# Slice 0 in halves over the hardware queues, slice 1 over the software queue: how a weight-gradient matmul starts

## The chip, the cores and the metric

One core of a Trainium2 chip. The metric is device time in microseconds (us) per execution. The kernel before takes 175.97 us (median of 6 runs, 175.87 to 176.45). In profiles, times count from the start of the profiled span, which is about 1.8 us shorter than the execution.

## The reference, cut to what matters

```python
batch, m, k, n = 16, 512, 1024, 768          # input [16,512,1024], grad_output [16,512,768], float32
grad_weight = np.einsum('bmk,bmn->kn', input, grad_output)     # [1024, 768]
```

Call the input X and the gradient G, both flattened to 8192 rows. The result is the transpose of X times G, a sum over 64 slices of 128 rows. One slice needs 12 matmuls of 512 columns: 8 "wide" ones (X's eight blocks of 128 columns against G's first 512 columns; A is blocks 0 to 3, B is 4 to 7) and 4 "narrow" ones (N: G's last 256 columns in two interleaved sets against X's two halves).

## The kernel before: the parts that matter

All inputs are float32 in HBM and are multiplied in bf16. The transfers that this kernel issues from GpSimd (the software queue, called the stream below) deliver bf16. Those that it issues from SyncE and ScalarE (the hardware queues) deliver float32, which VectorE (DVE) and ScalarE (ACT) round. Slice 0 comes that way, and X of slice 1. In the profile lines PE is TensorE, PEld its weight loads, POOL is GpSimd; a transfer "lands" when its last part has arrived.

```python
ORDER = ("A1! B1 N1 B2! N2 A2 N3! A3 B3 A4! B5 N5 B6! N7 A6 N8! A9! B10 N9 B12! N12! A12! "
         "B15 AB17! n17! AB26! n26! AB41! n41! AB47 A50! B50! N64!").split()
WARMUP = [512] * 10 + [128] * 2
# ... cut ...
xf = [head.tile([P, K], f32, name=f"xf{s}") for s in range(2)]
gf = head.tile([P, N], f32, name="gf")
nc.sync.dma_start(out=gf[:, 0:NA], in_=G[0:P, 0:NA])          # wide G of slice 0
nc.scalar.dma_start(out=xf[0], in_=X[0:P, :])                 # X of slice 0, whole rows of 4 KB
nc.sync.dma_start(out=gf[:, NA:N], in_=G[0:P, NA:N])          # narrow G of slice 0
nc.scalar.dma_start(out=xf[1], in_=X[P : 2 * P, :])           # X of slice 1
# ... warm-up matmuls on ones ...
for s in range(1, S):                                         # the software stream
    gt = xg.tile([P, N], bf16, name="gt")
    nc.gpsimd.dma_start(out=gt, in_=G[s * P : (s + 1) * P, :])
    if s > 1:
        xs[s] = xg.tile([P, K], bf16, name="xt")
        nc.gpsimd.dma_start(out=xs[s], in_=X[s * P : (s + 1) * P, :])
```

`ORDER` is the schedule of the matmuls. "B10" takes B up to slice 10, "!" closes the part: its four PSUM banks are evicted (copied or added into SBUF by DVE and ACT) and set free. The kernel uses eight banks, so two parts can be open at a time.

## Time and profile before

| what | before |
|---|---|
| span, TensorE busy | 174.3 us, 97% |
| first useful matmul | 5.32 us |
| last matmul starts | 171.25 us |
| stream | one slice (G and X) per 2.2 us |
| TensorE | one slice per 2.59 us (12 x 0.216) |

The profile's chain, timeline and landings are read in the prediction below.

### The profile page before, as it was taken

The page shows a single profiled execution, that of the slowest core. Times are in us where ns is not written, and L with a number is a line of the kernel's source. Part 1 is how long each engine was busy: PE and PEld are TensorE (multiplying, and loading weights), DVE is VectorE, ACT ScalarE, POOL GpSimd, SP SyncE. Part 2 cuts the span into 40 slices and gives each one's busy share as a digit, 9 for nine tenths or more (in the row PEclk, how much of TensorE's full clock was granted, in tenths as well). Part 3 has the DMA queues.
Part 4 walks back from the last instruction along what each step waited for, and adds up shares of the span by engine and source line. Part 5 has one row for each costly group of instructions (what it writes and reads, how often), then busy time and mean ns, then how long its engine had stood idle before and what let it go on. Part 6 is the DMA issues. An engine that isn't in the chain of part 4 may idle for free.

```text
span 174.3 us, 2013 instructions
## 1 busy us (share of the span) xinstructions
PE 169.9 (97%) x793; PEld 78.4 (45%) x808; DVE 61.3 (35%) x103; ACT 6.2 (4%) x12; POOL 66.7 (38%) x129
## 2 busy tenths in 40 slices
PE   8999999999999999999999999999999999999993
PEld 3444444444444444444444444444444444444463
DVE  0655582883940039300000662200560003931122
ACT  2640000000000000000000000000000000000000
POOL 7444434444444444444444444444274200000000
PEclk9999999999999999999999999999999999999999
DMA  5999999999999999999999999999999990085623
GB/s 192 276 208 209 207 209 208 208 208 209 207 208 209 207 208 210 207 209 209 206 209 208 208 210 207 207 209 208 207 209 209 207 202 11 0 190 160 170 86 120
DMA packets 25048, 33.35 MB, mean 191 GB/s; under 512 B 6480, under 2 KB 16592, under 8 KB 25040
## 3 DMA queue, kind: packets, MB, share of 16 engines
q0 software_dynamic: 18000, 28.65, 89.9%
q10 hardware_dynamic: 4448, 2.10, 4.7%
q1 hardware_dynamic: 2592, 2.49, 4.2%
q8 instruction: 6, 0.10, 0.2%
q14 instruction: 2, 0.02, 0.0%
HBM read 58.72 MB, written 3.15 MB: 355 GB/s over the span
## 4 chain that ended last, share of the span: by engine, by line
PE 97%; issue 0%; DVE 0%
PE bank L127 63%; PE bank L134 32%; PE bank L81 3%; DVE acc L118 0%
## 5 line engine op out<-in xcount | busy, mean ns | idle before, releaser
L127 PE MATMUL bank<-gt,xt 128*128 128x512 bf16 (+2 forms) x515 | 108.3, 367 | 0.5
L127 PEld LDWEIGHTS <-xt 128*128 128x128 bf16 x524 | 50.2, 98 | 57.2
L118 DVE TENSOR_TENSOR acc<-bank,acc 128x512 f32<-128x512 f32 (+2 forms) x62 | 37.9, 667 | 73.4 <-PE bank L127 72.9
L134 PE MATMUL bank<-xt,gt 128*128 128x512 bf16 x242 | 54.8, 379 | 0.3
L97 POOL DMA_DIRECT2D xt<-in_input_dram x62 | 33.1, 533 | 38.7 <-DMA xt<-in_input_dram 36.5
L92 POOL DMA_DIRECT2D gt<-in_grad_output_dram x63 | 33.8, 536 | 31.2 <-DMA gt<-in_grad_output_dram 24.9
L134 PEld LDWEIGHTS <-gt 128*128 128x128 bf16 x252 | 24.6, 98 | 29.7
L118 DVE TENSOR_TENSOR acct<-bank,acct 128x512 f32<-128x512 f32 x24 | 15.7, 682 | 30.0 <-PE bank L134 29.9
L81 PE MATMUL bank<-const-bfloat16-1.0 128*128 128x512 bf16 (+1 forms) x12 | 4.6, 574 | 0.8 <-PEq L263 0.8
L81 PEld LDWEIGHTS <-const-bfloat16-1.0 128*128 128x128 bf16 x12 | 1.6, 140 | 3.5 <-issue 3.5
L122 DVE COPY acc<-bank 128x512 f32<-128x512 f32 x4 | 2.7, 687 | 1.0 <-PE bank L127 1.0
L180 DVE STREAM_TRANSPOSE turned<-acct 128x512 f32<-128x512 f32 x4 | 2.9, 715 | 0.1
L127 PEld LDWEIGHTS <-x 128*128 128x128 bf16 x16 | 1.6, 98 | 1.9 <-DVE x L107 0.2
L107 DVE CAST g<-gf 128x256 bf16<-128x256 f32 x2 | 0.6, 290 | 4.7 <-DMA gf<-in_grad_output_dram 4.7
L124 ACT COPY acc<-bank 128x512 f32<-128x512 f32 x4 | 2.1, 589 | 1.3 <-PE bank L127 1.3
L127 PE MATMUL bank<-gt,x 128*128 128x512 bf16 x8 | 2.1, 379 | 0.0
L127 PE MATMUL bank<-g,x 128*128 128x512 bf16 x8 | 2.0, 398 | 0.0
L122 DVE COPY acct<-bank 128x512 f32<-128x512 f32 x2 | 1.3, 686 | 1.3 <-PE bank L134 1.3
L107 ACT CAST x<-xf 128x256 bf16<-128x256 f32 x4 | 1.4, 409 | 0.0
L107 ACT ACT_TABLE_LOAD x1 | 1.3, 1283 | 1.7 <-PEq L263 1.7
L124 ACT COPY acct<-bank 128x512 f32<-128x512 f32 x2 | 1.1, 588 | 1.5 <-PE bank L134 1.5
L107 DVE CAST x<-xf 128x256 bf16<-128x256 f32 (+1 forms) x5 | 1.0, 260 | 0.0
(8 smaller groups left out, 3.3 us busy)
## 6 DMA issues: line engine op xcount, KB each, us to landing
xt<-in_input_dram POOLq DMA_DIRECT2D x62, 256.0 KB, 8.5
gt<-in_grad_output_dram POOLq DMA_DIRECT2D x63, 192.0 KB, 8.5
out_dram<-acc SPq DMA_DIRECT2D x13, 128.0 KB, 2.7
xf<-in_input_dram ACTq DMA_DIRECT2D x2, 512.0 KB, 5.1
out_dram<-turned ACTq DMA_DIRECT2D x4, 256.0 KB, 3.4
gf<-in_grad_output_dram SPq DMA_DIRECT2D x1, 256.0 KB, 3.9
out_dram<-acc SPq DMA_DIRECT2D x1, 256.0 KB, 2.0
gf<-in_grad_output_dram SPq DMA_DIRECT2D x1, 128.0 KB, 4.7
```

The source lines that it names most:

```text
L81: nc.tensor.matmul(wps[:, 0:cols], ones, nc.const_aps.tensor(1.0, (P, cols), bf16), start=True, stop=True,)
L92: nc.gpsimd.dma_start(out=gt, in_=G[s * P : (s + 1) * P, :])
L97: nc.gpsimd.dma_start(out=xs[s], in_=X[s * P : (s + 1) * P, :])
L107: copy(out=dst[:, c0:c1], in_=src[:, c0:c1])
L118: nc.vector.tensor_add(out=dst, in0=src, in1=dst)
L122: nc.vector.tensor_copy(out=dst, in_=src)
L124: nc.scalar.copy(out=dst, in_=src)
L127: nc.tensor.matmul(bank, xs[s][:, k * P : (k + 1) * P], gwide[s][:, c0:c1], start=start, stop=stop)
L134: nc.tensor.matmul(bank, gnarrow[s].rearrange("p (r t) -> p t r", t=NT)[:, t], xs[s][:, h * NA : (h + 1) * NA], start=start, stop=stop,)
L180: nc.vector.transpose(out=turned[:, h * hb : (h + 1) * hb, :, t], in_=dst.rearrange("p (b r) -> p b r", r=SQ),)
```

## The change

The intent: TensorE starts on 256 KB of G and 256 KB of X instead of 512 KB of X, so the first useful matmul comes earlier; the warm-up is shortened to match. X of slice 1 no longer passes through the hardware queue and the two rounding engines but comes as bf16 by the software queue, its later half first, since B of slice 1 needs that one first. Narrow G is used before B.

```diff
-    "A1! B1 N1 B2! N2 A2 N3! A3 B3 A4! ...
+    "A1! N1 B2! N2 A2 N3! A3 B3 A4! ...
-WARMUP = [512] * 10 + [128] * 2
+WARMUP = [512] * 9 + [128] * 3
...
-    nc.scalar.dma_start(out=xf[0], in_=X[0:P, :])
+    nc.scalar.dma_start(out=xf[:, 0:NA], in_=X[0:P, 0:NA])
     nc.sync.dma_start(out=gf[:, NA:N], in_=G[0:P, NA:N])
-    nc.scalar.dma_start(out=xf[1], in_=X[P : 2 * P, :])
+    nc.scalar.dma_start(out=xf[:, NA:K], in_=X[0:P, NA:K])
...
-        if s > 1:
-            xs[s] = xg.tile([P, K], bf16, name="xt")
-            nc.gpsimd.dma_start(out=xs[s], in_=X[s * P : (s + 1) * P, :])
+        xs[s] = xg.tile([P, K], bf16, name="xt")
+        for c0, c1 in ((NA, K), (0, NA)) if s == 1 else ((0, K),):
+            nc.gpsimd.dma_start(out=xs[s][:, c0:c1], in_=X[s * P : (s + 1) * P, c0:c1])
...   (first rounding of G: DVE 304 columns, ACT 208, instead of 256 each;
...    X's four first blocks alternate between DVE and ACT; the rounding of narrow G moves ahead of the first eviction; slice 1's roundings are gone)
-        "N": Part(narrow_mm, [(t, h) for h in range(KH) for t in range(NT)], narrow_dst),
+        "N": Part(narrow_mm, [(t, h) for h in reversed(range(KH)) for t in range(NT)], narrow_dst),
```

More of the change, by code (lines that the diff above doesn't have):

```diff
@@ L17 @@
 ORDER = (
-    "A1! B1 N1 B2! N2 A2 N3! A3 B3 A4! B5 N5 B6! N7 A6 N8! A9! B10 N9 B12! N12! A12! "
+    "A1! N1 B2! N2 A2 N3! A3 B3 A4! B5 N5 B6! N7 A6 N8! A9! B10 N9 B12! N12! A12! "
     "B15 AB17! n17! AB26! n26! AB41! n41! AB47 A50! B50! N64!"
 ).split()
-WARMUP = [512] * 10 + [128] * 2
+WARMUP = [512] * 9 + [128] * 3
 XBUFS = 42
@@ L67 @@
     ctx.enter_context(tc.manual_schedule(engines={E.PE, E.DVE, E.Activation}))
-    xf = [head.tile([P, K], f32, name=f"xf{s}") for s in range(2)]
+    xf = head.tile([P, K], f32, name="xf")
     gf = head.tile([P, N], f32, name="gf")
     nc.sync.dma_start(out=gf[:, 0:NA], in_=G[0:P, 0:NA])
-    nc.scalar.dma_start(out=xf[0], in_=X[0:P, :])
+    nc.scalar.dma_start(out=xf[:, 0:NA], in_=X[0:P, 0:NA])
     nc.sync.dma_start(out=gf[:, NA:N], in_=G[0:P, NA:N])
-    nc.scalar.dma_start(out=xf[1], in_=X[P : 2 * P, :])
+    nc.scalar.dma_start(out=xf[:, NA:K], in_=X[0:P, NA:K])
     ones = nc.const_aps.tensor(1.0, (P, P), bf16)
@@ L92 @@
         nc.gpsimd.dma_start(out=gt, in_=G[s * P : (s + 1) * P, :])
+        xs[s] = xg.tile([P, K], bf16, name="xt")
+        for c0, c1 in ((NA, K), (0, NA)) if s == 1 else ((0, K),):
+            nc.gpsimd.dma_start(out=xs[s][:, c0:c1], in_=X[s * P : (s + 1) * P, c0:c1])
         gwide[s] = gt[:, 0:NA]
         gnarrow[s] = gt[:, NA:N]
-        if s > 1:
-            xs[s] = xg.tile([P, K], bf16, name="xt")
-            nc.gpsimd.dma_start(out=xs[s], in_=X[s * P : (s + 1) * P, :])
-    for s in range(2):
-        xs[s] = head.tile([P, K], bf16, name=f"x{s}")
+    xs[0] = head.tile([P, K], bf16, name="x0")
     g0 = head.tile([P, N], bf16, name="g0")
@@ L107, in round_by @@
         copy(out=dst[:, c0:c1], in_=src[:, c0:c1])
-    round_by("DVE", g0, gf, 0, 256)
-    round_by("ACT", g0, gf, 256, NA)
-    round_by("DVE", xs[0], xf[0], 0, P)
-    round_by("ACT", xs[0], xf[0], 2 * P, 4 * P)
-    round_by("DVE", xs[0], xf[0], P, 2 * P)
-    round_by("DVE", xs[0], xf[0], 4 * P, 6 * P)
-    round_by("ACT", xs[0], xf[0], 6 * P, 8 * P)
+    round_by("DVE", g0, gf, 0, 304)
+    round_by("ACT", g0, gf, 304, NA)
+    for k in range(0, KS // 2, 2):
+        round_by("DVE", xs[0], xf, k * P, (k + 1) * P)
+        round_by("ACT", xs[0], xf, (k + 1) * P, (k + 2) * P)
+    round_by("DVE", g0, gf, NA, N)
+    round_by("DVE", xs[0], xf, NA, 6 * P)
+    round_by("ACT", xs[0], xf, 6 * P, K)
     def add_out(dst, src):
@@ L172, in add_slice @@
             copy_out(dst, bank, i)
-            if s == 0 and i == 0:
-                round_by("DVE", g0, gf, NA, N)
         else:
@@ L210, in bank_by_bank @@
                 add_slice(part, i, s, s == first, s == upto - 1)
-    for i, step in enumerate(ORDER):
-        if i == 2:
-            round_by("DVE", xs[1], xf[1], 4 * P, 6 * P)
-            round_by("ACT", xs[1], xf[1], 6 * P, 8 * P)
-            round_by("DVE", xs[1], xf[1], 0, 2 * P)
-            round_by("ACT", xs[1], xf[1], 2 * P, 4 * P)
+    for step in ORDER:
         close = step.endswith("!")
```

## The prediction

> **What bounds the kernel now.** I read the page of the slowest core first, then TensorE's instructions in order of time, then the start of the timeline over all engines, then the landings of the first transfers.
>
> ```profile
> span 174.3 us, 2013 instructions
> ...
> PE 169.9 (97%) x793; PEld 78.4 (45%) x808; DVE 61.3 (35%) x103; ACT 6.2 (4%) x12; POOL 66.7 (38%) x129
> ...
> PE 97%; issue 0%; DVE 0%
> ```
>
> The chain that ended last is TensorE for 97% of the span. Nothing but matmuls stands on it, so the time is: the moment at which the first useful matmul starts, plus the matmuls at their pace, plus what they wait for on the way, plus the tail of add and store. In order of time:
>
> ```profile
> 0.78 4.64 PE L81 MATMUL bank<-const-bfloat16-1.0 128*128 128x512 bf16 x12 [0.78 <-PEq L263]
> 5.32 2.04 PE L127 MATMUL bank<-g,x 128*128 128x512 bf16 x8
> 7.20 1.03 PE L134 MATMUL bank<-x,g 128*128 128x512 bf16 x4
> 8.06 1.03 PE L127 MATMUL bank<-gt,x 128*128 128x512 bf16 x4
> ```
>
> The twelve warm-up matmuls of ones (line 81) run from 0.78, the useful work starts at 5.32. From 7.20 on every group of four starts 0.86 us after the last one (0.216 us per matmul), and no row of TensorE after that shows an idle time before it. So there is no wait in the body to remove; 768 x 0.2158 = 165.7 us of the 174.3 are fixed, and the change can only move the start. The first eight took 1.88 us instead of 8 x 0.216 = 1.73: the trace's clock record begins full rate at 5.63, and single starts are 5.324, 5.686, 5.903, then 0.216 apart. The warm-up matmuls lie 0.427 apart, so until 5.63 the array runs at half pace. What released the first one:
>
> ```profile
> 4.71 0.41 ACT L107 CAST g<-gf 128x256 bf16<-128x256 f32 x1 [1.76 <-DMA gf<-in_grad_output_dram]
> 4.71 0.29 DVE L107 CAST g<-gf 128x256 bf16<-128x256 f32 x1 [4.71 <-DMA gf<-in_grad_output_dram]
> 5.00 0.15 PEld L81 LDWEIGHTS <-const-bfloat16-1.0 128*128 128x128 bf16 x1 [0.28 <-issue]
> 5.04 0.71 ACT L107 CAST x<-xf 128x256 bf16<-128x256 f32 x2
> 5.04 0.56 DVE L107 CAST x<-xf 128x128 bf16<-128x128 f32 x3
> ...
> 5.32 1.55 PEld L127 LDWEIGHTS <-x 128*128 128x128 bf16 x8 [0.17 <-DVE x L107]
> ```
>
> Wide G of slice 0 lands, is rounded (4.71), then X of slice 0 lands and is rounded (5.04), then the first weights load at 5.32, 0.17 us late against the end of the warm-up (last start 5.104 plus 128 columns at half pace, 0.107: 5.21). The landings in the trace are 4.684 (G wide), 5.017 (X of slice 0), 5.844 (G narrow), 7.027 (X of slice 1), and on the software queue 7.492 (G1), 8.462 (G2), 9.698 (X2), then 2.2 us per slice, while TensorE takes 12 x 0.216 = 2.59 us per slice.
>
> **What the Trainium skill says.** "DMA: Bandwidth & Descriptors", section "Queues, rings and completion order": each DMA engine takes turns between queues at packet granularity. The packet records agree: a 2048-byte packet of G (84 ns) and a 4096-byte packet of X (159 ns) alternate, one pair in 235 to 243 ns, so X with its double rows gets two thirds of the rate. The same page, "Latency and other measured facts", gives about 1 us to the first byte of a software DMA; here the first software packet starts at 5.275, 4.0 us after its issue at 1.23, so I don't use that figure. "TensorE: Matmul & The Clock Gate", "What's actually happening": the array runs at half rate until a free-running window of 3413 ns has been busy. The trace agrees (0.427 against 0.216 us, full rate from 5.63) but one profile can't show whether the moment is fixed. "ScalarE: Activation LUTs", "What ACT_TABLE_LOAD costs": 186 ns + 0.833 ns per element, successors overlapping by 93 ns; for 256 columns that is 0.40, the trace has 0.405 and a start-to-start of 0.31.
>
> **The change part by part.**
>
> Transfers. Before, the first useful matmul stands behind 256 KB of G and 512 KB of X. After, it stands behind 256 KB and 256 KB. An engine has 8 rows of each; a pair costs 84 + 84 = 168 instead of about 238 ns. The first packets are slow to start (the DMA share is 0.25 and 0.79 in the second and third microsecond), so I count 7 pairs: 7 x 0.07 = 0.49 us. Wide G then lands at about 4.2, X's first half one packet later at about 4.3 (5.017 before).
>
> Rounding. DVE 304 columns: 0.22 at 128 and 0.29 at 256 give about 0.31; ACT 208: 0.36. DVE starts its next piece some 0.08 us before the end (5.04, 5.18, 5.32), so X block 0 starts at about 4.25 + 0.23 = 4.48, and its weights load 0.28 later, as before: 4.76. ACT's share of G ends at 4.61. X blocks 1 and 3 (ACT) are ready at 4.8 and 5.0, ahead of their matmuls.
>
> Warm-up. One 512 becomes a 128: 0.32 us less, it ends at 5.21 - 0.32 = 4.89. The data being ready at 4.76, the warm-up decides, and the first useful matmul starts at 4.89, 0.43 earlier.
>
> What that is worth. The clock still rises at 5.63, I take it, so the matmuls from 4.89 run at half pace: starts 4.89, 5.32, then 380 columns until 5.63 and 132 at full rate, so the third starts at 5.69 against 5.903. Only half of the 0.43 is kept: **0.21 us**.
>
> Second halves. X's later half and narrow G of slice 0 are needed by the fifth matmul now (narrow goes ahead of B and takes the later half first), at 5.69 + 2 x 0.216 = 6.12. Eight further pairs per engine (46 for a 1 KB row by the 84 ns for 2 KB, estimated, + 84 = 130 ns) after about 3.9: landing near 5.3, roundings (DVE 0.28 and 0.29, ACT 0.41) done by 5.75. Slack 0.35.
>
> Banks. B of slice 0 reuses A's banks at the ninth matmul, 6.98. DVE is free at 5.75, its two evictions (0.69, 0.68) end at 6.43 and 7.03, for matmuls 9 and 11 (6.98, 7.41); ACT's (0.59) at 6.4 and 6.9 for 7.20 and 7.63. They hold.
>
> Software queue. X of slice 1 goes ahead of G2 now; hardware bytes fall from 1408 to 896 KB. The bytes read from HBM up to the end of X2 stay the same (2688 KB), so if the engines are never idle X2 lands near 9.7 again. If instead the software queue can't start before 5.275, it finds the engines almost free: some 240 KB of hardware packets that shared the time after 5.275 are gone, 0.55 us. Then G1 lands at 6.95, X1's later half at 7.55 (half of the 1.236 between G2 and X2), its earlier half at 8.2, G2 at 9.15, X2 at 10.4. Needed, at the new pace: G1 and X1's later half at 7.85, the earlier half at 9.14, G2 and X2 at 10.44. It holds, by 0.05 in the worst place. From slice 3 on the order is the old one, with 0.7 us or more to spare.
>
> Tail: the same stores and transposes. The sum is -0.21 us: 175.9 - 0.2 = 175.7.
>
> **Rivals.** (1) Slice 1 or 2 comes late: the software queue starts after 5.275, or halves cost more than half. For: the slack is 0.05 to 0.3 us in this reading. Against: equal bytes to X2. It would give the gain back: 175.9 to 176.1. (2) The data are no faster, because the slow start and not the bytes decides the landings: TensorE idles from 4.89 to about 5.2, gain 0.05 us, 175.85. For: the low DMA share until 3.0. (3) The clock's rise moves. If it came with the work and not at a fixed moment, the full 0.43 would count: 175.5; if the changed warm-up missed a window, 3.4 us at half pace would cost 1.7: 177.6. Against the latter: the array is as busy as before, and three runs before lie within 0.16 us.
>
> **Range and chances.** The likely outcomes lie from 175.5 to 176.0; runs of one kernel spread by 0.16, and another chip may add 0.1 to 0.2: 175.3 to 176.1. Two per cent is 3.5 us, more than everything that happens before the third useful matmul could give; only (3) at its worst comes near on the slow side.
>
> **What would show it.** Right: first useful matmul near 4.9, second 0.43 later, full clock at 5.63, the third near 5.7, no idle time before matmuls of slices 1 and 2; X of slice 0 landing near 4.3 and 5.3. Wrong: an idle time on a DMA at slice 1 or 2 (rival 1), between warm-up and work (rival 2), a clock record elsewhere than 5.63 (rival 3), or evictions that hold up the ninth matmul.

## The result, and the profile after

The changed kernel takes 176.62 us (median of 6 runs, 176.20 to 176.75), before 175.97; the ratio is 1.0026 (95% interval 1.0009 to 1.0044). A ratio is the mean time of one kernel's runs over the mean of the other's in the same rounds, so it is not quite the ratio of the medians. The forecast was 175.7 with a range of 175.3 to 176.1: the direction was wrong, and the time lies outside the range.

The page of the changed kernel, its span and its chain (share of the span by engine, then by line):

```profile
span 174.4 us, 2027 instructions
...
PE 81%; DMA 15%; POOL 2%; issue 1%; DVE 0%; POOLq 0%
PE bank L127 54%; PE bank L134 27%; DMA xt<-in_input_dram 15%; POOL gt L92 1%; POOL xt L95 1%; DVE acc L118 0%; POOLq L255 0%
```

Before, the chain was matmuls for 97%. Now it is followed back through 15% of transfers of X: somewhere TensorE waited for the stream, and the chain goes over to it. TensorE in order of time (start, length of the group, idle time before it) shows where:

```profile
4.71 1.04 PE L127 MATMUL bank<-g,x 128*128 128x512 bf16 x4
5.86 1.04 PE L134 MATMUL bank<-x,g 128*128 128x512 bf16 x4
6.73 1.03 PE L127 MATMUL bank<-g,x 128*128 128x512 bf16 x4
7.59 1.03 PE L127 MATMUL bank<-gt,xt 128*128 128x512 bf16 x4
8.46 1.03 PE L134 MATMUL bank<-xt,gt 128*128 128x512 bf16 x4
9.32 1.03 PE L127 MATMUL bank<-gt,xt 128*128 128x512 bf16 x4
10.28 1.02 PE L134 MATMUL bank<-xt,gt 128*128 128x512 bf16 x4
...
29.46 1.03 PE L127 MATMUL bank<-gt,xt 128*128 128x512 bf16 x4
30.66 1.04 PE L127 MATMUL bank<-gt,xt 128*128 128x512 bf16 x4 [0.17 <-DMA xt<-in_input_dram]
```

The trace of before has no break at that place; the eight matmuls of slices 10 and 11 follow each other:

```profile
28.78 1.03 PE L134 MATMUL bank<-xt,gt 128*128 128x512 bf16 x4
29.64 1.89 PE L127 MATMUL bank<-gt,xt 128*128 128x512 bf16 x8
31.37 2.75 PE L134 MATMUL bank<-xt,gt 128*128 128x512 bf16 x12
```

The start went as planned: 4.71 instead of 5.32. A group of four takes 0.863 us, so each larger step is a wait: 0.28 us before 5.86 (the first four begin at 4.71, 4.93, 5.15, 5.36, so N could have begun at 5.58), 0.10 before 10.28 (slice 2), 0.34 before 30.66 (slice 11). Two more of 0.10 and 0.07 stand before slices 4 and 6. (The idle times in brackets are shorter than the steps, because the end of a matmul is modelled 0.16 us late.) The last matmul starts at 171.41 against 171.25: a lead of 0.62 us at the start has become a lag of 0.16.

The waits tell the same. Before and after, the rows of the weight loads that wait for a transfer or a rounding (us in total, times, longest):

```profile
PEld L127 <- DVE x L107: 0.2, 1, 0.2
```

```profile
PEld L127 <- DMA xt<-in_input_dram: 1.3, 3, 0.7
...
PEld L134 <- DVE x L106: 0.6, 1, 0.6
```

The landings of X in the trace of after: slice 0's halves at 4.339 and 5.350, slice 1's at 7.385 and 8.050, slice 2 at 10.240 (9.698 before), slice 11 at 30.613 (30.158 before). So the stream is 0.54 us late at slice 2 and 0.455 at slice 11, where before had 0.35 to spare.

The trace also shows the clock record beginning full rate at 4.38 us, not at 5.63 as before.

### The profile page after: what moved, and what is told of

The parts are those of the page before. It is cut to its first block, busy times and chain, and to the rows that moved or that the text cites. A ratio compares the mean times of both kernels' runs of the same rounds, so it can differ in the third digit from the quotient of the medians. Undisturbed runs are those within 1.5% of the kernel's fastest.

```text
span 174.4 us, 2027 instructions
## 1 busy us (share of the span) xinstructions
PE 170.6 (98%) x808; PEld 78.0 (45%) x808; DVE 61.1 (35%) x101; ACT 5.6 (3%) x11; POOL 67.7 (39%) x131
## 4 chain that ended last, share of the span: by engine, by line
PE 81%; DMA 15%; POOL 2%; issue 1%; DVE 0%; POOLq 0%
PE bank L127 54%; PE bank L134 27%; DMA xt<-in_input_dram 15%; POOL gt L92 1%; POOL xt L95 1%; DVE acc L118 0%; POOLq L255 0%
## 5 line engine op out<-in xcount | busy, mean ns | idle before, releaser
L127 PE MATMUL bank<-gt,xt 128*128 128x512 bf16 (+2 forms) x532 | 111.1, 368 | 0.2 <-DMA xt<-in_input_dram 0.2
L127 PEld LDWEIGHTS <-xt 128*128 128x128 bf16 x532 | 50.8, 98 | 58.9 <-DMA xt<-in_input_dram 1.3
L134 PE MATMUL bank<-xt,gt 128*128 128x512 bf16 x252 | 56.3, 379 | 0.0
L95 POOL DMA_DIRECT2D xt<-in_input_dram x64 | 34.0, 532 | 37.3 <-DMA xt<-in_input_dram 35.9
L81 PE MATMUL bank<-const-bfloat16-1.0 128*128 128x512 bf16 (+1 forms) x12 | 4.0, 516 | 0.8 <-PEq L255 0.8
L106 DVE CAST g<-gf 128x304 bf16<-128x304 f32 (+1 forms) x2 | 0.7, 374 | 4.3 <-DMA gf<-in_grad_output_dram 4.2
L134 PE MATMUL bank<-x,g 128*128 128x512 bf16 x4 | 1.0, 382 | 0.1
L127 PEld LDWEIGHTS <-x 128*128 128x128 bf16 x8 | 0.8, 97 | 0.7
L106 ACT CAST x<-xf 128x128 bf16<-128x128 f32 (+1 forms) x3 | 0.9, 330 | 0.4 <-DMA xf<-in_input_dram 0.4
L106 DVE CAST x<-xf 128x128 bf16<-128x128 f32 (+1 forms) x3 | 0.8, 291 | 0.1
```

The costliest lines, as they stand in the source:

```text
L81: nc.tensor.matmul(wps[:, 0:cols], ones, nc.const_aps.tensor(1.0, (P, cols), bf16), start=True, stop=True,)
L95: nc.gpsimd.dma_start(out=xs[s][:, c0:c1], in_=X[s * P : (s + 1) * P, c0:c1])
L106: copy(out=dst[:, c0:c1], in_=src[:, c0:c1])
L127: nc.tensor.matmul(bank, xs[s][:, k * P : (k + 1) * P], gwide[s][:, c0:c1], start=start, stop=stop)
L134: nc.tensor.matmul(bank, gnarrow[s].rearrange("p (r t) -> p t r", t=NT)[:, t], xs[s][:, h * NA : (h + 1) * NA], start=start, stop=stop,)
```

## The experiments

Three theories stood at the start: S, the software stream binds, at slice 11; C, the moment of the clock's rise makes the time; R, the wait of 0.28 us for the roundings before N of slice 0 costs. All kernels gave correct results. The times, with the kernel before in the same rounds (on three chips):

| run | what | median us (range) | before, median | ratio (95% interval) |
|---|---|---|---|---|
| e1_again | the changed kernel | 176.30 (176.10 to 176.69) | 175.94 | 1.0022 (1.0010 to 1.0035) |
| e2_whole_x1 | X of slice 1 whole | 176.32 (176.10 to 176.36) | 175.94 | 1.0018 (1.0005 to 1.0032) |
| e3_old_warmup | long warm-up | 176.47 (176.37 to 176.59) | 175.94 | 1.0030 (1.0017 to 1.0043) |
| e4_order | slice 11 later, first try | 176.92 (176.48 to 177.09) | 175.94 | 1.0050 (1.0037 to 1.0062) |
| e5_order2 | slice 11 later | 176.44 (176.10 to 176.87) | 175.95 | 1.0029 (1.0011 to 1.0046) |
| e6_before_x1_sw | before, X of slice 1 by software | 176.33 (176.07 to 176.65) | 175.95 | 1.0020 (1.0005 to 1.0034) |
| e7_before_again | before | 175.95 (175.84 to 176.08) | 175.95 | 0.9996 (0.9984 to 1.0008) |
| e8_best | e5 + e2 + N's halves swapped | 176.22 (175.95 to 176.36) | 175.95 | 1.0009 (0.9996 to 1.0022) |
| e9_before_late | before, 256 KB more in the stream | 176.77 (176.57 to 176.95) | 175.98 | 1.0041 (1.0029 to 1.0054) |
| e10_halves_only | change without the move of X1 | 177.18 (177.09 to 177.46) | 175.98 | 1.0071 (1.0057 to 1.0085) |
| e11_before_order2 | before, slice 11 later | 175.86 (175.81 to 176.41) | 175.98 | 0.9999 (0.9984 to 1.0015) |
| e12_after_same_chip | the changed kernel | 176.34 (176.15 to 176.74) | 175.98 | 1.0020 (1.0005 to 1.0034) |
| e13_hw_beside | e6 with a hardware load beside | 177.11 (2 runs) | 175.94 | 1.0064 (1.0035 to 1.0094) |
| e14_pool_later | change, software issues later | 177.10 (2 runs) | 175.94 | 1.0064 (1.0016 to 1.0112) |

And what the one traced run of each shows, in us. "Clock" is where the clock record begins full rate ("none": that trace has no such record); "last" is the start of the last matmul; "slow" is the excess of software packets up to 9.0 us over the usual time of packets of their size (98, 135 and 173 ns for 1, 1.5 and 2 KB), summed over 16 engines.

| run | first useful | clock | X2 lands | X11 lands | last | last - X11 | first software packet | slow |
|---|---|---|---|---|---|---|---|---|
| before | 5.32 | 5.63 | 9.70 | 30.16 | 171.25 | 141.09 | 5.28 | 0 |
| e7 (before) | 5.28 | 3.72 | 9.64 | 30.46 | 171.25 | 140.79 | 5.30 | 0 |
| e11 | 5.24 | 5.08 | 9.63 | 30.41 | 171.03 | 140.62 | 5.31 | 0.05 |
| after | 4.71 | 4.38 | 10.24 | 30.61 | 171.41 | 140.79 | 4.64 | 2.1 |
| e1 (after) | 4.89 | 4.89 | 10.45 | 31.10 | 171.89 | 140.79 | 4.71 | 5.3 |
| e12 (after) | 4.66 | 4.14 | 10.55 | 31.16 | 171.95 | 140.79 | 4.61 | 3.1 |
| e2 | 4.89 | 3.58 | 9.91 | 30.70 | 171.50 | 140.79 | 4.90 | 0.07 |
| e3 | 5.21 | 5.20 | 10.38 | 31.03 | 171.82 | 140.79 | 4.57 | 5.0 |
| e4 | 4.89 | 6.16 | 10.37 | 31.07 | 171.87 | 140.80 | 4.61 | 2.5 |
| e5 | 4.89 | 6.43 | 10.23 | 30.78 | 171.43 | 140.65 | 4.75 | 2.6 |
| e6 | 5.36 | 4.81 | 10.34 | 30.75 | 171.54 | 140.79 | 4.39 | 4.7 |
| e8 | 4.89 | none | 10.03 | 30.40 | 171.30 | 140.91 | 4.58 | 2.2 |
| e9 | 5.25 | 5.54 | 9.62 | 31.17 | 171.96 | 140.79 | 5.24 | 0 |
| e10 | 4.65 | 3.98 | 9.73 | 30.65 | 171.93 | 141.29 | 4.75 | 0.1 |
| e13 | 5.24 | 6.37 | 11.00 | 31.58 | 172.38 | 140.79 | 5.34 | 0.02 |
| e14 | 4.89 | 6.15 | 11.69 | 31.56 | 172.67 | 141.11 | 4.68 | 5.5 |

### e1: the changed kernel again

No edit.

> The changed kernel unaltered, for a second trace and a wider set of times. Theory S (software stream binds): the first matmul of slice 11 again waits for its X, which lands near 30.6 us against 30.16 before; waits of 0.1 us or less at slices 2, 4, 6; time 176.2 to 176.75, 0.2 to 0.5 above the kernel before in the same rounds. Theory C (clock): the time follows the moment at which the array reaches full rate (4.38 us in the first trace after, 5.63 in the one before); if it comes after 6.5 us, the wait at slice 11 is gone and the time is above 176.4. Theory R (rounding): the wait of 0.28 us before the narrow matmuls of slice 0 is what costs; it should then be seen at every clock.

As theory S has it. The two traces of the changed kernel differ by 0.49 us in time (176.20 and 176.69), by 0.49 in the landing of X of slice 11, and both end 140.79 us after it. The clock rose at 4.38 in one and 4.89 in the other, in both no later than the first useful matmul (4.71 and 4.89), so it can't make the 0.49. The wait at N of slice 0 is 0.11 here instead of 0.28, in the slower run: R falls.

### e2: X of slice 1 in one piece

```diff
-        for c0, c1 in ((NA, K), (0, NA)) if s == 1 else ((0, K),):
+        for c0, c1 in ((0, K),):
```

> The changed kernel with X of slice 1 as one software transfer of 2 KB rows instead of two of 1 KB rows. Theory S with the small rows as the cause: X of slice 1 takes 1.2 us instead of 1.78, everything behind it lands 0.4 to 0.55 us earlier, X of slice 11 near 30.15, the wait there shrinks from 0.34 to under 0.1; time 0.2 to 0.4 us under the changed kernel's, about the kernel before. If slice 1 itself is then waited for, by under 0.2 us. Theory R: no change against the changed kernel.

X of slice 1 took the 1.2 us expected (G1 lands at 6.48, X1 at 7.70) and X of slice 2 came 0.54 us earlier than in e1. Slice 11 landed at 30.70, 0.40 earlier than in e1, which is within the 0.4 to 0.55 expected, but not at the 30.15 expected; the wait there was 0.54 and not under 0.1, and the median did not move (176.32 against 176.30). The small rows are at most a part of the cause.

### e3: the longer warm-up

```diff
-WARMUP = [512] * 9 + [128] * 3
+WARMUP = [512] * 10 + [128] * 2
```

> The changed kernel with the longer warm-up of before (ten of 512, two of 128 columns), so that the useful work starts up to 0.32 us later (0.1 to 0.2 at full rate). Theory S: the later start is swallowed by a shorter wait at slice 11; time equal to the changed kernel within 0.1 us. A theory in which the start sets the end: 0.1 to 0.3 us slower than the changed kernel.

The useful work starts 0.32 us later than in e1, the end follows X of slice 11 as before (140.79). But the wait at slice 11 is not the shorter one that was expected (0.61 us, 0.62 in e1). The lead of e1 is gone earlier: there the first matmul of slice 2 starts at 10.49, here at 10.43, in both 0.04 after its X has landed. The median is 0.17 over e1's, a little more than expected but inside e1's range, and the traced runs go the other way (171.82 against 171.89). The earlier start, the gain that the change was made for, is swallowed by the stream: in e1 at slice 2 already, in the trace after by the waits before N and at slices 2, 4, 6 and 11 together.

### e4 and e5: ask for slice 11 later

e4 edited the schedule like this:

```diff
-    ... A9! B10 N9 B12! N12! A12! B15 AB17! ...
+    ... A9! N9 B11! N11! A12! B14 AB17! ...
```

> The changed kernel with a schedule that asks for slice 11 16 matmuls (3.4 us) later: B and N close at 11 instead of 12, A still at 12, B goes on to 14. Same matmuls, same evictions. Theory S: the wait of 0.34 us at slice 11 is gone, at most 0.13 us reappears at slice 16; time 0.2 us or more under the changed kernel. Theory R or a slower tail: no change.

Slower, not faster. TensorE of e4 in order of time:

```profile
25.38 1.03 PE L134 MATMUL bank<-xt,gt 128*128 128x512 bf16 x4
26.24 1.01 PE L127 MATMUL bank<-gt,xt 128*128 128x512 bf16 x3
27.47 3.83 PE L127 MATMUL bank<-gt,xt 128*128 128x512 bf16 x17 [0.22 <-DVE acc L118]
31.13 1.89 PE L134 MATMUL bank<-xt,gt 128*128 128x512 bf16 x8
```

The wait for X is gone, but B now opens four matmuls after A closed, on banks that DVE has not yet emptied: two waits of 0.20 and 0.38 us for evictions. My edit had moved N ahead of B, which I had not meant to matter. That its end stands 140.80 us after X of slice 11 is chance: nothing in it waits for that slice. e5 keeps the order of N and B:

```diff
-    ... A9! B10 N9 B12! N12! A12! B15 AB17! ...
+    ... A9! B10 N9 B11! N11! A12! B14 AB17! ...
```

> The changed kernel with slice 11 asked for 16 matmuls (3.4 us) later, this time without moving the order of N and B before it: B and N close at 11, A still at 12, B goes on to 14. Theory S (the wait for X of slice 11 sets the end): that wait is gone and no eviction wait takes its place (it did in the first attempt, e4); what may remain are 0.1 us at slices 2, 4, 6 and up to 0.3 us at slice 16 when the stream runs late. The last matmul then starts 140.5 us or less after X of slice 11 landed instead of 140.79; time 0.1 to 0.4 us under the changed kernel. If the time stays, the stream binds at slice 16 as well or the theory falls.

The traced run has no wait at all after the first matmuls and ends 140.65 us after X of slice 11: at 30.78 + 140.79 = 171.57 it would have ended with the wait, at 171.43 it did. What held it back is the clock, which rose at 6.43 only: the first three useful matmuls ran at half rate throughout. The median of all runs (176.44) does not show the gain, though. It could show little: in the three traces of the changed kernel, with the wait at slice 11 behind them, slice 16 has only 0.25 to 0.26 us left, and a matmul that waits starts 0.05 after its landing. So with slice 11 out of the way slice 16 would bind in its place, and the end could come 0.2 us earlier at most, which is less than the 0.77 by which e5's runs spread. In the traced run of e5 slice 16 had 0.13 us left (X lands at 41.79, its matmul starts at 41.92); e14 below does wait there, 0.15 us. What held the runs up to 176.87 no trace shows. So taking the wait away did not win the time back, and for that half of the proof there are only the traces.

### e6, e7: which part of the change makes the stream late

e6 takes the kernel before and moves X of slice 1, whole, to the software queue:

```diff
-    nc.scalar.dma_start(out=xf[1], in_=X[P : 2 * P, :])
...
-        if s > 1:
-            xs[s] = xg.tile([P, K], bf16, name="xt")
-            nc.gpsimd.dma_start(out=xs[s], in_=X[s * P : (s + 1) * P, :])
+        xs[s] = xg.tile([P, K], bf16, name="xt")
+        nc.gpsimd.dma_start(out=xs[s], in_=X[s * P : (s + 1) * P, :])
...   (slice 1's roundings removed)
```

> The kernel before with one part of the change alone: X of slice 1 on the software queue as one whole transfer, its roundings gone; X of slice 0 whole on the hardware queue, old warm-up, old order. Theory S with small rows as the cause of the late stream: with whole rows everywhere, the stream keeps the pace of before; X of slice 2 lands at 9.7 to 9.9 us and X of slice 11 within 0.15 us of the kernel before on this chip; time equals before within 0.1 us. If moving X of slice 1 itself delays the stream (not its halves), X of slice 11 is 0.3 us or more later and the time 0.1 us or more longer.

> The kernel before unaltered, for a second trace. No wait after the start; X of slice 11 lands 0.2 to 0.35 us before its first matmul; last matmul near 171.2 us; time 175.8 to 176.1.

The move alone, with whole rows, costs what the whole change costs: 1.0020. X of slice 2 lands at 10.34 against 9.64 in e7 on the same chip, X of slice 11 at 30.75 against 30.46. So the second branch of the expectation held (its 0.3 us at slice 11 just missed, with 0.29), and the halves are not needed to explain it. e7 brought a surprise: there the kernel before waits at slice 11 too, 0.18 us, and ends 140.79 us after that landing. Two things add up to it: the clock rises early (3.72), so TensorE is 0.18 us ahead of the first trace of before, and X of slice 11 lands 0.30 us later than there. Either alone would have fitted into the 0.35. That 0.30 arises after slice 8 (slices 9 to 11 take 7.59 us, 7.23 in the first trace), not at the start. The kernel before was already at the balance between start and stream, and a slightly later stream is enough to tip it.

### e8: what the experiments pointed to, together

```diff
-    ... B12! N12! A12! B15 AB17! ...
+    ... B11! N11! A12! B14 AB17! ...
-        for c0, c1 in ((NA, K), (0, NA)) if s == 1 else ((0, K),):
+        for c0, c1 in ((0, K),):
-        "N": ... for h in reversed(range(KH)) ...
+        "N": ... for h in range(KH) ...
```

> The changed kernel with what the experiments so far point to: X of slice 1 whole, slice 11 asked for later, and N of slice 0 with X's earlier half first so that it need not wait for the later half. Theory S: no wait at slice 11; the wait of 0.27 us before N of slice 0 is gone, but X of slice 1 landing near 7.7 us then holds slice 1 by up to 0.25 us; matmul 12 starts near 7.75 against 8.06 before, last matmul near 170.95 if nothing else waits; time 175.6 to 175.8, 0.1 to 0.3 us under before.

No wait is left in the traced run, yet it ends at 171.30, not 170.95: the first four useful matmuls took 1.50 us (4.89 to 6.39) instead of 0.86, so the array was at half rate until about 6.2 (2048 columns = 1.2 x 1290 ns + 2.4 x 210 ns). 1.0009: this ties with before.

### e9: the kernel before with nothing but a later stream

```diff
             nc.gpsimd.dma_start(out=xs[s], in_=X[s * P : (s + 1) * P, :])
+            if s == 2:
+                spare = head.tile([P, NA], bf16, name="spare")
+                nc.gpsimd.dma_start(out=spare, in_=X[0:P, 0:NA])
```

> The kernel before with nothing altered but the stream: one more software transfer of 256 KB (X of slice 0, first half, into a tile that nobody reads) behind X of slice 2, about 0.62 us of the stream. Everything before slice 3 is untouched. Theory S: X of slice 11 lands near 30.8 to 31.1 us (30.16 and 30.46 in the two traces of before), its first matmul waits 0.2 to 0.6 us, the last matmul starts 140.79 us after that landing, time 0.3 to 0.6 us over before: a late stream alone makes what the change made. Rival: if the lateness at slice 11 costs nothing, time as before.

This is the experiment that leaves the start, the halves and the roundings alone. X of slice 2 lands at 9.62 as before, X of slice 11 at 31.17, and TensorE of e9 stands there:

```profile
28.81 1.03 PE L137 MATMUL bank<-xt,gt 128*128 128x512 bf16 x4
29.67 1.03 PE L130 MATMUL bank<-gt,xt 128*128 128x512 bf16 x4
31.21 1.04 PE L130 MATMUL bank<-gt,xt 128*128 128x512 bf16 x4 [0.52 <-DMA xt<-in_input_dram]
```

The step from 29.67 to 31.21 is 1.54 us instead of 0.863, a wait of 0.68. It ends at 31.17 + 140.79 = 171.96 and takes 1.0041 of before. A late stream is sufficient. (It is 1.01 us later at slice 11 than in the first trace of before; in the three traces of the changed kernel that is 0.455 to 1.0.)

### e10: the change without the move

```diff
+    xf1 = head.tile([P, K], f32, name="xf1")
+    nc.scalar.dma_start(out=xf1, in_=X[P : 2 * P, :])      # behind slice 0's halves
...   (X of slice 1 out of the software stream; its four roundings as in the kernel before)
```

> The changed kernel with X of slice 1 back on the hardware queue, whole, behind the halves of X of slice 0, and rounded by VectorE and ScalarE as before: the halves, the new order, the uneven rounding and the shorter warm-up without the move to the software queue. If the move makes the stream late (slow software packets between 5 and 7 us, seen in every run with it and in neither trace of before): no slow packets, X of slice 2 lands 9.6 to 9.9 us, X of slice 11 within 0.25 us of before; useful work starts at 4.7 to 4.9; time between before minus 0.2 and before plus 0.15. If the halves of slice 0 are what makes it late: X of slice 11 is 0.3 us or more behind before's and the time 0.2 us or more over before.

The stream is nearly punctual at first (slow packets: 0.1 us; X of slice 2 at 9.73); slice 11, at 30.65, is 0.2 to 0.5 us behind the traces of before, lost between slices 8 and 11 (7.68 us). But the time is the worst of the three full calls, for a reason that neither branch named:

```profile
4.65 1.04 PE L130 MATMUL bank<-g,x 128*128 128x512 bf16 x4
5.80 1.04 PE L137 MATMUL bank<-x,g 128*128 128x512 bf16 x4
6.68 1.03 PE L130 MATMUL bank<-g,x 128*128 128x512 bf16 x4
8.74 1.04 PE L130 MATMUL bank<-gt,x 128*128 128x512 bf16 x4 [1.03 <-DVE x L109]
```

The software queue starts at 4.75 here (5.28 in before) and shares the engines with X of slice 1, which lands at 8.36 instead of 7.03; slice 1 then waits 1.2 us. So the halves want X of slice 1 off the hardware queue, and that move delays the stream: the parts of the change belong together, and the second pays back what the first wins.

### e11, e12: the later slice 11 in the kernel before, and the changed kernel beside it

e11 is the schedule edit of e5 on the kernel before; e12 has no edit.

> The kernel before with slice 11 asked for 16 matmuls later, as in e5. Theory S: before itself waits at slice 11 when the clock rises early (0.18 us in its second trace), so the order takes up to 0.2 us off in such runs and nothing in the others; time before minus 0.1, give or take 0.1; no wait at slice 11 in the trace.

> The changed kernel unaltered, on the chip of e9 to e11 for comparison. Time 0.2 to 0.5 us over before; last matmul 140.79 us after X of slice 11 landed; slow software packets between 5 and 7 us.

e11's trace has no wait and ends earliest of all (171.03); its median is the lowest (175.86), its ratio 0.9999. It is not shown to be faster than before, so there is no version here that beats both kernels. e12 repeats the changed kernel's lag: 1.0020, last matmul 140.79 us after X of slice 11.

### e13, e14: why the stream is late

Read from the packet records, bytes of the input packets that had ended by a time, in KB (software packets count twice, since they write bf16 and read float32):

```
by (us)       5.0    5.5    6.0    6.5    7.0    8.0   10.0
e11 (before) 1014   1222   1427   1629   1831   2223   3043
e12 (after)   962   1166   1306   1430   1594   1970   2781
```

The lag is 52 KB at 5.0, grows to 237 KB at 7.0 and then nearly stays (253 at 8.0, 262 at 10.0). At the 404 KB/us of e11 after 7.0 that is some 0.13 us from the hardware phase and 0.45 us from the stretch 5.5 to 7.0, where the slow packets lie. The slow packets are not the whole of it: their 3.1 us, over 16 engines, are 0.20 us; the small rows (256 packets of 98 ns instead of 128 of 173) make another 0.18, an estimate from these durations; and the engines were idle more (a share of 1.04 against 1.15 in the first lines below). X of slice 2 lands 0.92 us later in e12 than in e11, so an average over the engines leaves about 0.3 us of it unexplained. The view of the 16 DMA engines in stretches of 1 us (the last three columns: granted clock, DMA share, GB/s written), first before, then e12:

```profile
6.00:7.00 1.00, 1.00 (x7) 0.41 (x6) 1.00 (x3) 0.90 (x2) 0.00 (x0) 1.00 1.15 226
7.00:8.00 1.00, 1.00 (x6) 0.47 (x5) 0.78 (x3) 0.79 (x3) 0.22 (x1) 1.00 1.18 213
```

```profile
6.00:7.00 1.00, 1.00 (x6) 0.49 (x5) 0.91 (x2) 0.66 (x2) 0.40 (x1) 1.00 1.04 152
7.00:8.00 1.00, 0.94 (x6) 0.24 (x4) 0.00 (x0) 0.00 (x0) 0.15 (x2) 1.00 1.19 204
```

In that microsecond the changed kernel writes 152 GB/s where the software stream alone otherwise makes 204 to 213. Two more runs asked under which condition.

```diff
 # e13, on e6: a hardware load nobody reads, where X of slice 1 was
+    nc.scalar.dma_start(out=spare, in_=X[P : 2 * P, :])
 # e14, on the changed kernel: GpSimd busy before its first issue
+    nc.gpsimd.memset(spare, 0.0)            # 128 x 1024, float32
```

> e6 (kernel before with X of slice 1 whole over the software queue) with a hardware load of 512 KB beside it that nobody reads, in the place that X of slice 1 had. If the software queue is slow only where it is alone on the engines early on: no slow packets (under 0.2 us of excess in all, e6 had over 4 us), and everything lands 1.27 us (512 KB) later than the kernel before would have it: X of slice 2 near 10.9. If slow packets come with X of slice 1 itself: 1 us or more of excess again. The time is longer than before either way (the stream carries 512 KB more): last matmul 140.79 us after X of slice 11.

> The changed kernel with a memset of 128x1024 on GpSimd ahead of its first issue, so that the software transfers are issued about 1 us later. If the queue drains before its descriptors are far enough ahead, later issues shift the first software packet and the slow packets with it, and the stream is 0.5 us or more later. If the first software packet still follows the last hardware one (4.6 to 5.0 us), issue is not what starts the queue, and the time is that of the changed kernel within 0.2 us.

e13: with hardware packets beside it the software queue starts at 5.34 instead of 4.39 and has no slow packets (0.02 us of excess against 4.7 in e6), X of slice 2 lands at 11.00. So it is not X of slice 1 as such. e14: the first issue moved from 1.23 to 1.63 us only, and the first software packet did not move (4.68). The slow packets came to 5.5 us, hardly more than in e1 (5.3), but X of slice 2 came at 11.69, against 10.24 to 10.55 in the three traces of the changed kernel; slice 1 waited for its X (0.78 us, from 8.11 to 8.89), and the time went to 177.10. So neither branch of its expectation holds whole: in this one trace the issue doesn't set when the queue starts, yet an issue 0.4 us later made the stream over 1.1 us later. Both fit a queue that begins to drain before its descriptors are far enough ahead, but no record shows the descriptors, e2 had next to no slow packets without any such help, and in e9 some appear around 10 us, where the queue had long been running. That mechanism stays open. One rival is weakened by the traces: DVE's roundings run at that time (4.18 to 5.79 in after), but in e10 they stand at the same times (4.13 to 5.75) and the slow packets come to 0.1 us, so they are not enough by themselves.

## Why the prediction was wrong, point by point

**What bounds the kernel.** Half right. The prediction said that the time is the start plus the matmuls plus waits, and "there is no wait in the body to remove". In that trace there was none; but the body had a second bound close behind, the stream at slice 11 with 0.35 us to spare, and e7 shows the kernel before waiting there in a run with an early clock. (That trace has a later stream as well, by 0.30 us.) No wait is not the same as room.

**Transfers, roundings, start.** Right. G landed at 4.16 (said 4.2), X's halves at 4.34 and 5.35 (4.3, 5.3), the start at 4.71 with an early clock and at 4.89 in the traces where the warm-up ended at half rate (e4, e5, e8, e14), as said. Roundings were mis-sized in one place: DVE's rounding of narrow G and of X's later half took 0.43 and 0.42 us, not 0.28 and 0.29. They still ended at 5.79, where 5.75 was said. The wait of 0.28 us before N comes from the other side: with the early clock N could begin at 5.58, not at 6.12. It is not what set the end: in e1 it is 0.11 and the run is longer.

**The clock.** "The clock still rises at 5.63, I take it" was wrong. Over the traces it rises anywhere from 3.58 to 6.43 us. So an earlier start keeps half or all of its lead by luck. (It is not what made the two traced runs of the changed kernel differ by half a microsecond; that was the stream, see e1.) It is not what made the change slower: with the clock at 4.38 the trace after had the better half of that luck, against 5.63 before.

**Banks.** Right: no eviction held up the ninth matmul.

**Software queue, the step that failed.** The prediction took two readings for slice 2, 9.7 from equal bytes and 10.4 in the worst case, and preferred no wait. 10.24 was measured. That it fell between the two is luck in part, since the terms were others: the software queue started at 4.64, not 5.275, G of slice 1 landed at 6.27 (6.95 in the worst case), and X's two halves took 1.78 us, not 1.24. Then it said: "From slice 3 on the order is the old one, with 0.7 us or more to spare." This is the step that is wrong. I had compared landings and starts up to slice 7 and stopped; slice 11 had 0.35 in the very same trace and slice 16 had 0.55. The 0.7 was also read from the kernel before, and the lateness of up to 0.7 in the same paragraph would have used it up: in the trace after, slices 4 and 6 wait too, by 0.10 and 0.07. At slice 11 the stream was 0.455 us late and TensorE still 0.18 ahead (the four matmuls before start at 29.46, 29.64 before), against 0.35 spare; with the 0.05 from landing to start that is the wait of 0.34, and from there the end is the landing plus 140.79 us whatever the start was. Put into the sum: 30.61 + 140.79 = 171.40, against 171.25 before, +0.15 us, which is what the best runs of after show (176.20 against 176.04 in the profiled runs); runs with a later stream (31.10, 31.16) show +0.65 to +0.7 (176.69, 176.74).

**The equal-bytes argument** failed as well: the bytes ahead of X of slice 2 are the same, but not the pace. The move of X of slice 1 alone (e6) made it 0.70 us late.

**Rivals.** Rival 1 had the right kind (a late software queue, halves that cost more than half) and the wrong size: it was put at 175.9 to 176.1. Its slice 2 did wait, 0.10 us in after, 0.30 in e1 and 0.25 in e12, but it was slice 11 that set the end. Rival 3's mechanism is real, its harm is not seen. Rival 2 did not occur.

## What to carry to other kernels

When a profile shows no wait, list the distance between each landing and its first use through the whole run before moving any transfer: the smallest distance, not the first ones, is the room that a change to the start has, and one trace is not enough to know it (slice 11 had 0.35 us in one trace of before and a wait in another). The place behind it counts too: slice 16 left e5 no more than 0.2 us to gain. Where a schedule takes data in jumps, an earlier start only moves the need earlier, and once one landing binds, the end is that landing plus a constant (140.79 us here, in nine of the sixteen traces, and by chance in e4, to within 0.01), which is a quick test of what binds. Equal bytes ahead of a transfer don't mean an equal landing when they change queues.

## What the Trainium skill lacked or had wrong

- "DMA: Bandwidth & Descriptors", section "Latency and other measured facts", gives about 1 us to the first byte of a software DMA. Here the first software packet came 3.2 to 4.1 us after its issue, with hardware transfers queued (issue at 1.23, packet at 4.39 to 5.34), and delaying the issue by 0.4 us left it at 4.68 (e14).
- The same page, section "Queues, rings and completion order", has each engine take turns between the queues for which it has work. In the trace after, the software queue gets no turn until the hardware queues run out: the first completions of the last hardware transfer stand at 4.637, 4.670 and 4.690 us, the first software packets at 4.643, 4.676 and 4.696. In the trace before it starts at 5.275 with hardware packets still running until 6.75. Whether the software queue had work for the engines earlier no record shows, and what decides its start no page says.
- No page gives durations for the slow software packets: 1 KB packets of usually 98 ns that take up to 445 ns in the trace after and 633 in e1, 2 KB packets of usually 173 ns that take up to 811 in e6, in sum 2 to 5.5 us of excess over 16 engines, mostly between 5 and 7 us, where X of slice 1 goes over the software queue (e2 excepted), and 0.1 us or less in e10 and e13, where hardware packets run beside it.
- "TensorE: Matmul & The Clock Gate", section "What's actually happening", agrees: a free-running window of 3.41 us means that the rise differs from run to run, and it lay between 3.58 and 6.43 us in these traces, a spread of 2.85, and at 5.63 and 3.72 in the two traces of the kernel before. The page gives ±500 ns for the moment of the change; here it was more.
- No page tells what a 16 KB instruction fetch does to a stream. One starts between 23.85 and 25.26 us in each of the sixteen traces and takes 0.89 to 0.98 us on its engine. In fifteen of them slices 9 to 11 took 7.14 to 7.68 us instead of 3 x 2.2 (7.15 in the trace after, 7.43 in e1, which makes 0.28 of the 0.49 us between their landings of slice 11). In e14 they took 6.63. That the fetch is the cause was not tested, and e14 shows that it doesn't always cost.
